# Decoder block on one core: the feed-forward's seven products regrouped, their sums kept in PSUM, and the last output row cut 512, 256, 256

## The chip, the core and the metric

One NeuronCore of a Trainium2 chip runs the whole program; the other cores are idle. The metric is the device time of one execution in microseconds. Before the change it was 758.20 us, the median of three runs (758.01 to 758.51). Lower is better. The output is compared with the reference in float32.

## What is computed

One decoder block on x of 512 tokens by 1024 channels. Cut to what matters here:

```
p   = x @ W_in + b_in                      # projections for two token mixers and their gates
m   = sigmoid(g_A) * y_A + sigmoid(g_B) * y_B   # y_A: gated mixing in chunks, y_B: gated linear attention
h   = layer_norm(alpha * x + m @ W_out)
f   = square(relu(h @ W_ff1)) @ W_ff2      # 1024 -> 4096 -> 1024
out = layer_norm(alpha * h + f)
```

The change is in the feed-forward, above all in the product with `W_ff2`, and in two small places beside it.

## The kernel before

**Every float32 product is three passes.** `split` (L88) writes a number as a rounded part `hi` (ScalarE's cast, L89) and a rest `lo` (VectorE's subtraction, L90). TensorE then sums hi·hi, hi·lo and lo·hi in one PSUM bank (`passes`, L196). Weights come in chunks of 128x1024 (512 KB), one DMA each on SyncE's queue (L111), into raw buffers, and are split into `wh` and `wl`, which have seven buffers each (`W_BUFS`), so that splitting runs up to seven chunks ahead of TensorE. `load_to`, `sum_to` and `split_to` (L102 to L143) drive this along a list of chunks that `_stream` (L1114) writes out.

**The stages, in order.** The first q and k products on the `head` array (L272); a small low-rank product `pa` whose weights are the tile `als` (L283 to L290, L327); the projections for u, v, q, k, the gates and the two mixers (up to about 365 us); the output projection and the first layer norm; from about 412 us the feed-forward.

**The feed-forward.** Hidden units come in 8 blocks of 512. A hidden job (`hidden`, L918) is 24 matmuls of 512 columns, and ScalarE squares its relu into the tile `F`. Two blocks make a pair: `F` then holds a 512-token by 1024-hidden matrix a, cut in 2 by 2 quarters, a(i,j) with i the token half and j the hidden block; the matching rows of `W_ff2` are cut in quarters b(i,j), i the hidden block and j the output half. For the first three pairs (`PAIRS`) the product a·b is made of seven products of quarters instead of eight (Strassen's scheme). `operand` (L935) makes the sum of quarters of a that a product needs, in the tile `d`, and splits it into `oh`, `ol`; `sum_to` makes the sums of quarters of b in place in the raw buffers (L124). Each product is 24 matmuls of 512 columns (L986), 12 for each half t of its 256 tokens. TensorE's order is written out: a hidden job of the next pair, a product, a hidden job, a product, and so on. `keep` (L955) takes each product out of PSUM into an SBUF sum of its own, `acc[m]`: for the first pair a ScalarE copy (L961), or VectorE with alpha·h added (L959); for later pairs a VectorE addition (L963). `together` (L993) combines the seven sums into the four quarters of the output `bufB`, partly among the last products, partly among the output pieces.

**The end.** The fourth pair is an ordinary product (L1077): for each of four 128-token rows, pieces of 512 and 512 columns, and for the last row pieces of 512, 384 and 128 columns. Each piece is 24 matmuls, then VectorE adds it to `bufB` (L1078) and takes the statistics (L1079). When a row is complete follow the aggregate (L1084), the reciprocal root on GpSimd (L1086), four operations for the layer norm (L1089, L1093) and two DMAs out.

**What sets the order.** TensorE, VectorE, ScalarE and GpSimd run in the order in which the program's functions issue instructions, except in the first stage, where only TensorE is fixed and the other engines are ordered by the framework. SyncE's queue is always ordered by the framework, and waits at its head hold up what stands behind. A tile that takes over another's memory waits until that one is done with.

Of the kernel before, what the change touches and what calls it, by code (L numbers as in the profile page):

```python
# [15 lines left out]
P = 128  # L16
# [30 lines left out]
def hybrid_block(  # L47
# [50 lines left out]
    raws, chunks, kept = {}, {}, {}  # L98
    lanes, ring = {0: rpool}, {lane: [] for lane in LANES}
    state = {"load": 0, "sum": 0, "split": 0}  # L100

    def load_to(n):  # L102
        while state["load"] < min(n, NCHUNK):
            i = state["load"]
            kind, lane, key, news = STREAM[i]
            if news is not None:
                ends = ring[lane]
                if len(ends) >= LANES[lane] and ends[-LANES[lane]] >= state["split"]:
                    break
                raw = lanes[lane].tile([P, 1024], F32, name=f"raw{i}", tag="raw")  # L110
                nc.sync.dma_start(raw, w_all[news])  # L111
                kept.setdefault(key, []).append(raw)
                users = [j for j in range(i + 1, NCHUNK) if STREAM[j][2] == key]
                users = [j for n_, j in enumerate(users) if all(STREAM[x][3] is None for x in users[:n_])]
                ends.append(max([i] + (users if key else [])))
            raws[i] = kept[key][-1:] if kind == "one" else kept[key][-2:]
            state["load"] = i + 1

    def sum_to(n):
        while state["sum"] < min(n, state["load"]):  # L120
            i = state["sum"]
            raw, *other = raws[i]
            if other:
                nc.vector.tensor_tensor(raw, raw, other[0], op=ALU.add if STREAM[i][0] == "sum" else ALU.subtract)  # L124
            state["sum"] = i + 1

    def split_to(n):
        n += n > ASIDE
        while state["split"] < min(n, NCHUNK):
            i = state["split"]  # L130
            load_to(i + 1)
            if i != ASIDE:
                hi = wpool.tile([P, 1024], F32R, name=f"wh{i}", tag="wh")
                lo = wpool.tile([P, 1024], F32R, name=f"wl{i}", tag="wl")
            else:
                hi, lo = (a[:, 4:6, :].rearrange("p k t -> p (k t)") for a in (xh, xl))
            sum_to(i + 2)
            raw = raws[i][0]
# [4 lines left out]
        load_to(n + sum(LANES.values()) if 1 in lanes else n + RAW_BUFS)  # L143

# [105 lines left out]
    for i in range(4):  # L250
        raws[i] = [None]
# [31 lines left out]
    als_ = gt.tile([P, 1536], F32R, name="als", tag="qt", bufs=QT_BUFS)  # L283
    nc.vector.memset(als_.bitcast(F32), 0.0)
    als = []
    for k, o in enumerate(ALS_AT):
        als.append(als_[:, 192 * k + o : 192 * k + o + P])
        a4 = als[k].rearrange("p (r m) -> p r m", r=4)
        split(a4[:, 0, 0:RANK], a4[:, 3, 0:RANK], wal[:, k, :])
        nc.scalar.copy(a4[:, 1:3, 0:RANK], a4[:, 0:1, 0:RANK].bitcast(F32).broadcast_to([P, 2, RANK]))  # L290
# [32 lines left out]
    def low_rank():  # L323
        pa = ps_a.tile([P, 512], F32, name="pa", tag="aux")
        for k in range(KT):
            for i, xx in enumerate((xh, xl)):
                nc.tensor.matmul(  # L327
                    pa, als[k], xx[:, k, :], start=(k == 0 and i == 0), stop=(k == KT - 1 and i == 1)
                )
# [573 lines left out]
    xp = pool(tail, "xp", side="right")  # L903
    acc = {m: xp.tile([P, 2, 512], F32, name=f"acc{m}") for m in (1, 2, 5)}
    quarter = lambda a, i, j: a[:, 2 * i : 2 * i + 2, 512 * j : 512 * j + 512]
    for m, i, j in ((7, 0, 0), (3, 0, 1), (4, 1, 0), (6, 1, 1)):
        acc[m] = quarter(bufB, i, j)
    fp = pool(tail, "fp", side="right", bufs=2)
    seven = ExitStack()
    lanes[1] = pool(seven, "rpool2", side="right", bufs=LANES[1])  # L910
    op = pool(seven, "op", side="left", bufs=2)
    sub = lambda o, x_, y_: nc.vector.tensor_tensor(o, x_, y_, op=ALU.subtract)  # L912
# [21 lines left out]

    def operand(F, p, m):  # L935
        a = lambda i, j: F[:, j - 1, :, (i - 1) * 256 : i * 256]
        x_, *y_ = {
            5: (a(1, 2), a(1, 1)),
            1: (a(1, 1), a(2, 2)),
            3: (a(1, 1),),  # L940
            4: (a(2, 2),),
            6: (a(2, 1), a(1, 1)),
            7: (a(1, 2), a(2, 2)),
            2: (a(2, 1), a(2, 2)),
        }[m]
        if y_:
            d_ = op.tile([P, 4, 256], F32, name=f"d{p}_{m}", tag="d", bufs=1)
            sub(d_, x_, y_[0])
            x_ = d_
# [5 lines left out]
    def keep(p, m, t, ps):  # L955
        dst = acc[m][:, t, :]
        if p == 0 and m in (6, 7):
            h = quarter(bufA, *((1, 1) if m == 6 else (0, 0)))[:, t, :]
            nc.vector.scalar_tensor_tensor(dst, h, ALPHA, ps, op0=ALU.mult, op1=ALU.add)  # L959
        elif p == 0:  # L960
            nc.scalar.copy(dst, ps)  # L961
        else:
            nc.vector.tensor_add(dst, dst, ps)  # L963

    made = {}

    def seven_products(F, p, F_next):
# [4 lines left out]
        def job(n):  # L972
            m = ORDER[n]
# [4 lines left out]
            hi, lo = made.pop((p, n))  # L978
            u0 = take_chunks(2)
            for t in range(2):  # L980
                tsl = slice(t * P, (t + 1) * P)
                ps = ps_m.tile([P, 512], F32, name=f"m{p}_{m}_{t}", tag="ps")
                for k in range(4):
                    wh, wl = (c.rearrange("p (k n) -> p k n", k=2)[:, k % 2, :] for c in chunks[u0 + k // 2])
                    for i, (s_, m_) in enumerate(passes(hi[:, k, tsl], lo[:, k, tsl], wh, wl)):
                        nc.tensor.matmul(ps, s_, m_, start=(k == 0 and i == 0), stop=(k == 3 and i == 2))  # L986
                    if t and k % 2:
                        split_to(u0 + k // 2 + 1 + W_BUFS)
                keep(p, m, t, ps)
# [3 lines left out]
    def together(m, t, terms, h=None):  # L993

        z = acc[m][:, t, :]
        for sign, n in terms:
            nc.vector.tensor_tensor(z, z, acc[n][:, t, :], op=ALU.add if sign > 0 else ALU.subtract)
        if h:
            nc.vector.scalar_tensor_tensor(
                z, quarter(bufA, *h)[:, t, :], ALPHA, z, op0=ALU.mult, op1=ALU.add  # L1000
            )
# [35 lines left out]
    for n, product in enumerate(seven_products(F, PAIRS - 1, None)):  # L1037
# [6 lines left out]
        if ORDER[n] == 4:  # L1044
            together(7, 0, ((1, 4),))
        if ORDER[n] == 1:
            together(7, 0, ((1, 1),))
# [4 lines left out]
    together(7, 0, ((-1, 5),))  # L1052
    later = {
        (0, 0): [(6, 0, ((1, 3),)), (3, 0, ((1, 5),), (0, 1))],
        (0, 1): [(7, 1, ((1, 4), (1, 1), (-1, 5))), (6, 1, ((1, 3),)), (3, 1, ((1, 5),), (0, 1))],
        (1, 0): [(4, t, ((1, 2),), (1, 0)) for t in range(2)],
        (1, 1): [(6, t, ((1, 1), (-1, 2))) for t in range(2)],
    }
# [7 lines left out]
    for t in range(NT):  # L1066
        tsl = slice(t * P, (t + 1) * P)
        row, z = bufA[:, t, :], bufB[:, t, :]
        pieces = ((0, 512), (512, 512)) if t < NT - 1 else ((0, 512), (512, 384), (896, 128))
        for pi, (c0, n) in enumerate(pieces):  # L1070
# [9 lines left out]
            for part in later.get((t, pi), ()):  # L1080
                together(*part)
# [32 lines left out]
def _stream():  # L1114
# [4 lines left out]
    out = [("one", 0, None, None)] * 4 + [("one", 0, None, c) for c in range(n)]  # L1119
# [3 lines left out]
    take = lambda k: [("one", 0, None, next(f1_jobs)) for _ in range(k)]  # L1123

    def operand(p, m, h):
        b = lambda i, j: f2 + 8 * p + 2 * (2 * (i - 1) + j - 1) + h
        kind, c = {
            2: ("one", b(1, 1)),
            6: ("sum", b(1, 2)),
            3: ("sum", b(2, 2)),  # L1130
            5: ("one", None),
            7: ("sum", b(2, 1)),
            4: ("sum", b(1, 1)),
            1: ("less", b(2, 2)),
        }[m]
        return (kind, h, (p, h), c)
# [6 lines left out]
    out += [("one", 0, None, f2 + 8 * PAIRS + c) for c in range(8 * (DF // 1024 - PAIRS))]  # L1143
# [81 lines left out]
```

## Time and profile before

| | |
|---|---|
| median of three runs | 758.20 us |
| the profiled execution | 757.96 us, of which 756.2 us from first to last instruction |
| TensorE busy | 747.2 us, 3498 matmuls |
| VectorE busy | 492.8 us, 618 instructions |
| ScalarE busy | 349.5 us, 472 instructions |
| mean granted TensorE clock | 0.997 |

The page's first part gives each engine's busy time and its share of the span. A row of the timeline gives the start of an instruction, its duration, the engine, the line, and output<-inputs with the shape. For TensorE the duration of one matmul is longer than the distance from one start to the next, since matmuls are pipelined; the distance is what counts for the time. A row of the chain of work that ended last gives the start, the length of the stretch, the engine, what it worked on, and how many instructions. A row of the waits gives who waited for whom, the total, how often, and the longest.

### The profile page before, as it was taken

The numbers are of one execution on the slowest core, as the hardware profiler recorded it, in microseconds if no ns is written. First come the engines' busy times: TensorE is split into PE (matmuls) and PEld (weight loads), VectorE is DVE, ScalarE is ACT, GpSimd is POOL, SyncE is SP. The second block draws the span as 40 slices with busy tenths as digits, with TensorE's granted clock in tenths as the row PEclk, the third lists the DMA queues.
The fourth block names the chain that finished last, engine by engine and source line by source line (L and its number), as shares of the span: only waits on it lengthen the run. The fifth ranks groups of instructions, "written<-read, shape, count | busy, mean of one in ns | idle before, by whom it ended". The sixth has DMA issues, their size and how long they took to land.

```text
span 756.2 us, 8829 instructions
## 1 busy us (share of the span) xinstructions
PE 747.2 (99%) x3498; PEld 626.8 (83%) x3498; DVE 492.8 (65%) x618; ACT 349.5 (46%) x472; POOL 29.8 (4%) x60
## 2 busy tenths in 40 slices
PE   9999999999999999999999999999999999999996
PEld 7878888888888888888888988888888888888885
DVE  8478876676575554435458544874677667777995
ACT  7475744363254735444222544454644444445300
POOL 1000000000000102000002000000000000000011
PEclk9999999999999999999999999999999999999998
DMA  8623422222142131432341423444234333534111
GB/s 341 208 73 125 137 77 80 84 84 84 36 141 75 56 126 56 144 107 84 98 158 33 171 62 107 139 140 140 86 137 141 137 112 112 164 114 166 58 56 55
DMA packets 25465, 85.15 MB, mean 113 GB/s; under 512 B 3088, under 2 KB 3344, under 8 KB 25424
## 3 DMA queue, kind: packets, MB, share of 16 engines
q1 hardware_dynamic: 25280, 84.33, 32.4%
q8 instruction: 27, 0.44, 0.2%
q10 hardware_dynamic: 144, 0.26, 0.1%
q14 instruction: 14, 0.11, 0.1%
HBM read 82.48 MB, written 2.10 MB: 112 GB/s over the span
## 4 chain that ended last, share of the span: by engine, by line
PE 96%; issue 1%; DVE 1%; DMA 0%; POOL 0%; DVEq 0%; POOLq 0%
PE f L691 22%; PE ps L213 17%; PE m L986 15%; PE f L1077 6%; PE gb L691 6%; PE r L691 6%; PE ga L691 6%; PE u L691 6%; PE qk L691 3%; PE first L272 3%; PE sc L519 2%; PE pm L744 1%; PE po L553 1%; PE po L557 1%; PE po L555 1%
## 5 line engine op out<-in xcount | busy, mean ns | idle before, releaser
L90 DVE TENSOR_TENSOR wl<-raw,wh 128x1024 fp32r<-128x1024 f32 x141 | 171.2, 1222 | 99.2 <-ACT wh L89 97.7
L89 ACT CAST wh<-raw 128x1024 fp32r<-128x1024 f32 x141 | 145.7, 1044 | 51.1 <-PE ps L213 23.7
L691 PE MATMUL f<-xh,wh 128*128 128x512 f32 (+1 forms) x288 | 105.4, 366 | 0.0
L691 PE MATMUL f<-xl,wh 128*128 128x512 f32 (+1 forms) x288 | 105.3, 365 | 0.0
L691 PE MATMUL f<-xh,wl 128*128 128x512 f32 (+1 forms) x288 | 105.2, 365 | 0.0
L986 PE MATMUL m<-wh,oh 128*128 128x512 f32 x168 | 65.4, 389 | 0.0
L986 PE MATMUL m<-wl,oh 128*128 128x512 f32 x168 | 65.4, 389 | 0.0
L986 PE MATMUL m<-wh,ol 128*128 128x512 f32 x168 | 65.4, 389 | 0.0
L691 PEld LDWEIGHTS f<-xh,wl 128*128 128x128 f32 x288 | 54.3, 189 | 8.8
L691 PEld LDWEIGHTS f<-xh,wh 128*128 128x128 f32 x288 | 54.3, 189 | 8.7
L691 PEld LDWEIGHTS f<-xl,wh 128*128 128x128 f32 x288 | 54.3, 189 | 8.6
L213 PE MATMUL ps<-wh,xh 128*128 128x512 f32 x128 | 50.4, 394 | 0.0
L213 PE MATMUL ps<-wh,xl 128*128 128x512 f32 x128 | 49.8, 389 | 0.0
L213 PE MATMUL ps<-wl,xh 128*128 128x512 f32 x128 | 49.8, 389 | 0.0
L915 ACT ACTIVATE F<-f 128x512 f32<-128x512 f32 (+1 forms) x28 | 15.0, 536 | 70.7 <-PE f L691 70.7
L124 DVE TENSOR_TENSOR raw<-raw,raw 128x1024 f32<-128x1024 f32 x30 | 36.6, 1221 | 9.1 <-DMA raw<-in_w_all 9.1
L986 PEld LDWEIGHTS m<-wh,ol 128*128 128x128 f32 x168 | 31.5, 188 | 6.6
L986 PEld LDWEIGHTS m<-wh,oh 128*128 128x128 f32 x168 | 31.5, 188 | 6.6
L986 PEld LDWEIGHTS m<-wl,oh 128*128 128x128 f32 x168 | 31.5, 188 | 6.5
L89 ACT CAST oh<-d 128x1024 fp32r<-128x1024 f32 x15 | 15.7, 1049 | 36.4 <-DVE d L912 36.4
L90 DVE TENSOR_TENSOR ol<-d,oh 128x1024 fp32r<-128x1024 f32 x15 | 18.4, 1225 | 16.7 <-ACT oh L89 16.7
L213 PEld LDWEIGHTS ps<-wh,xl 128*128 128x128 f32 x128 | 24.0, 188 | 5.1
(231 smaller groups left out, 1477.1 us busy)
## 6 DMA issues: line engine op xcount, KB each, us to landing
raw<-in_w_all SPq DMA_DIRECT2D x136, 512.0 KB, 3.3
bufB<-in_head SPq DMA_DIRECT2D x4, 512.0 KB, 7.9
xr<-in_x SPq DMA_DIRECT2D x8, 256.0 KB, 3.6
out<-bufA SPq DMA_DIRECT2D x8, 256.0 KB, 2.0
bufA<-in_head SPq DMA_DIRECT2D x3, 512.0 KB, 5.3
brow<-in_b_in SPq DMA_DIRECT2D x4, 256.0 KB, 6.4
g<-in_ln_g SPq DMA_DIRECT2D x2, 512.0 KB, 4.0
b<-in_ln_b SPq DMA_DIRECT2D x2, 512.0 KB, 4.9
```

The costliest lines, as they stand in the source:

```text
L89: nc.scalar.copy(hi, src)
L90: nc.vector.tensor_tensor(lo, src, hi.bitcast(F32), op=ALU.subtract)
L124: nc.vector.tensor_tensor(raw, raw, other[0], op=ALU.add if STREAM[i][0] == "sum" else ALU.subtract)
L213: nc.tensor.matmul(ps, s_, m_, start=(k == 0 and i == 0), stop=(k == KT - 1 and i == 2))
L272: nc.tensor.matmul(first[e], s_, m_[:, k, :], start=(k == 0 and i == 0), stop=(k == KT - 1 and i == 2))
L519: nc.tensor.matmul(sc[:, c, 0:192], pr.kt[:, jc * P : (jc + 1) * P], pr.qt[:, jc, :], start=True, stop=True)
L553: nc.tensor.matmul(po, pr.AT[:, j, c, :], vs, start=True, stop=(c == 0))
L555: nc.tensor.matmul(po, pr.QI[:, j, c * P : (c + 1) * P], pr.S[j], start=False, stop=True)
L691: nc.tensor.matmul(ps, s_, m_, start=(k == 0 and i == 0), stop=(k == KT - 1 and i == 2))
L915: nc.scalar.activation(dst, ps, AF.Relu)
L986: nc.tensor.matmul(ps, s_, m_, start=(k == 0 and i == 0), stop=(k == 3 and i == 2))
L1077: nc.tensor.matmul(ps, s_, m_, start=(f == 0 and i == 0), stop=(f == 7 and i == 2))
```

## The change

**Another form of the seven products.** The order of the products becomes 1, 2, 5, 6, 3, 7, 4 (`ORDER`), and with it what each multiplies (Winograd's scheme). On a's side four sums are made in place in one tile `d`: s1 = a(2,1)+a(2,2) for product 5, s2 = s1-a(1,1) for 6, s4 = a(1,2)-s2 for 3, s3 = a(1,1)-a(2,1) for 7; products 1, 2 and 4 take a(1,1), a(1,2) and a(2,2) as they are. On b's side t1 = b(1,2)-b(1,1) for 5, t2 = b(2,2)-t1 for 6, b(2,2)-b(1,2) for 7, b(2,1)-t2 for 4; products 1, 2 and 3 take b(1,1), b(2,1) and b(2,2).

**Kept raw weights.** Four tiles A0, A1, B0, B1 (`held`; 0 and 1 are the halves of a quarter) keep b(1,1), t1 and t2, and b(2,2), across products; the rest of the loads share three raw buffers. A pair still loads 12 chunks of `W_ff2`: b(1,2) and b(2,1) twice. Product 3 needs no load; before, it was product 5.

**Two accumulators in PSUM.** Products 1, 6, 7, 4 are summed one on top of the other in the two banks `mx`, products 5 and 3 in the two banks `mv`; product 2 has banks of its own. After each product VectorE adds the state of its accumulator to one quarter of `bufB`; for the first pair products 1, 5, 6 and 4 bring alpha·h along. The separate sums `acc` in SBUF and all of `together` are gone, and ScalarE copies nothing out any more. A product that goes on in an accumulator may only start when VectorE has read it for the product before.

**Beside it.** The low-rank weights `als` are built in one of the `wh` buffers by fewer, larger instructions. The last row's pieces are 512, 256, 256. The memory reserved for descriptors that GpSimd would write is cut to 1024 bytes a partition, which makes room for the four kept tiles.

```diff
-ORDER = (2, 6, 3, 7, 4, 1, 5)
+ORDER = (1, 2, 5, 6, 3, 7, 4)
...
+            _, own, dst, _, less = STREAM[i]
+            if dst is not None:
+                raw = held[dst]
+                if less:
+                    x_, y_ = (held[a] if a else kept[i] for a in less)
+                    nc.vector.tensor_tensor(raw, x_, y_, op=ALU.subtract)
+                kept[i] = raw
...
-    als_ = gt.tile([P, 1536], F32R, name="als", tag="qt", bufs=QT_BUFS)
-    nc.vector.memset(als_.bitcast(F32), 0.0)
-    als = []
-    for k, o in enumerate(ALS_AT):
-        als.append(als_[:, 192 * k + o : 192 * k + o + P])
-        a4 = als[k].rearrange("p (r m) -> p r m", r=4)
-        split(a4[:, 0, 0:RANK], a4[:, 3, 0:RANK], wal[:, k, :])
-        nc.scalar.copy(a4[:, 1:3, 0:RANK], a4[:, 0:1, 0:RANK].bitcast(F32).broadcast_to([P, 2, RANK]))
+    als = wpool.tile([P, KT, 4, 32], F32R, name="als", tag="wh")
+    nc.vector.memset(als.bitcast(F32), 0.0)
+    split(als[:, :, 0, 0:RANK], als[:, :, 3, 0:RANK], wal)
+    for r_ in (1, 2):
+        nc.scalar.copy(als[:, :, r_, 0:RANK], als[:, :, 0, 0:RANK].bitcast(F32))
...
+    def accumulators(m, name):
+        if m in (1, 6, 7, 4):
+            if m == 1:
+                x_ = ps_s.tile([P, 2, 512], F32, name=f"mx{name}", tag="sc")
+                sums["x"] = [x_[:, t, :] for t in range(2)]
+            return sums["x"], m == 1
+        if m in (5, 3):
+            if m == 5:
+                sums["v"] = [ps_a.tile([P, 512], F32, name=f"mv{name}_{t}", tag="aux") for t in range(2)]
+            return sums["v"], m == 5
+        return [ps_m.tile([P, 512], F32, name=f"m{name}_{t}", tag="ps") for t in range(2)], True
...
+                    nc.tensor.matmul(
+                        ps,
+                        s_,
+                        m_,
+                        start=(begins and k == 0 and i == 0),
+                        stop=(k == 3 and i == 2),
+                        skip_group_check=True,
+                    )
...
+            dst = quarter(bufB, *GOES[m])[:, t, :]
+            if p == 0 and m in NEW:
+                h = quarter(bufA, *GOES[m])[:, t, :]
+                nc.vector.scalar_tensor_tensor(dst, h, ALPHA, ps, op0=ALU.mult, op1=ALU.add)
+            else:
+                nc.vector.tensor_add(dst, dst, ps)
...
-        pieces = ((0, 512), (512, 512)) if t < NT - 1 else ((0, 512), (512, 384), (896, 128))
+        pieces = ((0, 512), (512, 512)) if t < NT - 1 else ((0, 512), (512, 256), (768, 256))
...
-    nc = bacc.Bacc("TRN2", target_bir_lowering=False, num_devices=1)
+    nc = bacc.Bacc("TRN2", target_bir_lowering=False, num_devices=1, dynamic_dma_scratch_size=1024)
```

Three places show what moves. The first is VectorE in the third pair. Before, this is the stretch around product 3: the rest `wl` of a chunk, the operand of product 7 (`d_7`, `ol_7`), product 3 taken out in two halves, and among them sums and rests of later chunks.

```order
L90 TENSOR_TENSOR wl_5005<-raw_4851,wh_5004 128x1024
L912 TENSOR_TENSOR d_7_5013<-F_4195 128x1024
L90 TENSOR_TENSOR ol_7_5016<-d_7_5013,oh_7_5015 128x1024
L963 TENSOR_TENSOR bufB<-bufB,m_3_0_5019 128x512
L90 TENSOR_TENSOR wl_5041<-raw_4884,wh_5040 128x1024
L124 TENSOR_TENSOR raw_4932<-raw_4932,raw_5011 128x1024
L90 TENSOR_TENSOR wl_5053<-raw_5009,wh_5052 128x1024
L963 TENSOR_TENSOR bufB<-bufB,m_3_1_5033 128x512
```

After the change this is the stretch around product 7 of the third pair, on whose accumulator `mx` product 4 goes on after one hidden job:

```order
L88 TENSOR_TENSOR wl_5173<-raw_5100,wh_5172 128x1024
L88 TENSOR_TENSOR ol_4_5179<-F_4149,oh_4_5178 128x1024
L991 TENSOR_TENSOR bufB<-bufB,mx_1_4799 128x512
L88 TENSOR_TENSOR wl_5202<-raw_5130,wh_5201 128x1024
L88 TENSOR_TENSOR wl_5214<-raw_5142,wh_5213 128x1024
L991 TENSOR_TENSOR bufB<-bufB,mx_1_4799 128x512
```

Here neither a sum of a's quarters nor a sum of b's quarters stands before the accumulator is read. The second place is VectorE's end, the last row's pieces, with `f_3_...` the pieces by their first column. Before:

```order
L1078 TENSOR_TENSOR bufB<-bufB,f_3_512_5631 128x384
L1079 BN_STATS st_3_2367<-bufB 128x6
L1078 TENSOR_TENSOR bufB<-bufB,f_3_896_5658 128x128
L1079 BN_STATS st_3_2367<-bufB 128x6
L1084 BN_AGGR mv_l_5685<-st_3_2367 128x2
```

After:

```order
L1073 TENSOR_TENSOR bufB<-bufB,f_3_512_5537 128x256
L1074 BN_STATS st_3_2347<-bufB 128x6
L1073 TENSOR_TENSOR bufB<-bufB,f_3_768_5564 128x256
L1074 BN_STATS st_3_2347<-bufB 128x6
L1077 BN_AGGR mv_l_5591<-st_3_2347 128x2
```

Only the widths differ, and with them the widths of the 48 matmuls in front. The third place is SyncE's queue early in the program, where the first layer norm's two rows `g` and `b` (broadcast to 128 partitions) now stand among the chunk loads; before, they stood some 45 rows further on. Before, the place reads:

```order
L111 DMA raw_385<-in_w_all 128x1024
L111 DMA raw_387<-in_w_all 128x1024
L111 DMA raw_429<-in_w_all 128x1024
L111 DMA raw_431<-in_w_all 128x1024
L111 DMA raw_534<-in_w_all 128x1024
```

After:

```order
L116 DMA raw_365<-in_w_all 128x1024
L116 DMA raw_367<-in_w_all 128x1024
L179 DMA g_2352<-in_ln_g 128x1024
L179 DMA b_2354<-in_ln_b 128x1024
L116 DMA raw_409<-in_w_all 128x1024
L116 DMA raw_411<-in_w_all 128x1024
L116 DMA raw_514<-in_w_all 128x1024
```

The two rows moved ahead, and every chunk load behind them is two places later in the queue.

More of the change, by code (lines that the diff above doesn't have):

```diff
@@ L36 @@
 RAW_BUFS = 3
-LANES = {0: RAW_BUFS, 1: 2}
 PAIRS = 3
-ORDER = (2, 6, 3, 7, 4, 1, 5)
+ORDER = (1, 2, 5, 6, 3, 7, 4)
 LEVELS = (32, 8, 2)
-ALS_AT = (0, 4, 48, 24, 12, 40, 56, 2)
 WARM = 9
@@ L96, in hybrid_block @@
     ASIDE = NCHUNK - 3
-    raws, chunks, kept = {}, {}, {}
-    lanes, ring = {0: rpool}, {lane: [] for lane in LANES}
+    chunks, kept, ring = {}, {}, []
+    held, held_to = {}, {}
     state = {"load": 0, "sum": 0, "split": 0}
@@ L104, in load_to @@
             i = state["load"]
[L105 to L108, printed above, removed]
+            c, own, *_ = STREAM[i]
+            if c is not None and own is None:
+                if len(ring) >= RAW_BUFS and ring[-RAW_BUFS] >= state["split"]:
                     break
[L110 to L116, printed above, removed]
+                kept[i] = rpool.tile([P, 1024], F32, name=f"raw{i}", tag="raw")
+                ring.append(i)
+            elif c is not None:
+                if "pool" not in held or held_to.get(own, -1) >= state["split"]:
+                    break
+                kept[i] = held[own] = held["pool"].tile([P, 1024], F32, name=f"raw{i}", tag=own)
+                held_to[own] = max(j for j in range(i, min(i + 40, NCHUNK)) if STREAM[j][3] == STREAM[i][3] and own in STREAM[j][2:])
+            if c is not None:
+                nc.sync.dma_start(kept[i], w_all[c])
             state["load"] = i + 1
@@ L121, in sum_to @@
             i = state["sum"]
-            raw, *other = raws[i]
-            if other:
-                nc.vector.tensor_tensor(raw, raw, other[0], op=ALU.add if STREAM[i][0] == "sum" else ALU.subtract)
+            _, own, dst, _, less = STREAM[i]
[5 more added lines that the diff above has]
+                kept[i] = raw
             state["sum"] = i + 1
@@ L137, in split_to @@
             sum_to(i + 2)
-            raw = raws[i][0]
+            raw = kept.pop(i, None)
             if raw is not None:
@@ L142, in split_to @@
             state["split"] = i + 1
-        load_to(n + sum(LANES.values()) if 1 in lanes else n + RAW_BUFS)
+        load_to(n + RAW_BUFS + 2)
     xh = xpool.tile([P, KT, T], F32R, name="xh")
@@ L248, in hybrid_block @@
         nc.tensor.matmul(wu[:, :P], ones, ones, start=True, stop=True)
-    for i in range(4):
-        raws[i] = [None]
     state["load"], state["sum"] = 4, 4
@@ L327, in low_rank @@
                 nc.tensor.matmul(
-                    pa, als[k], xx[:, k, :], start=(k == 0 and i == 0), stop=(k == KT - 1 and i == 1)
+                    pa, als[:, k].rearrange("p r m -> p (r m)"), xx[:, k, :], start=(k == 0 and i == 0), stop=(k == KT - 1 and i == 1)
                 )
@@ L895, in hybrid_block @@
     )
-    xp = pool(tail, "xp", side="right")
-    acc = {m: xp.tile([P, 2, 512], F32, name=f"acc{m}") for m in (1, 2, 5)}
     quarter = lambda a, i, j: a[:, 2 * i : 2 * i + 2, 512 * j : 512 * j + 512]
-    for m, i, j in ((7, 0, 0), (3, 0, 1), (4, 1, 0), (6, 1, 1)):
-        acc[m] = quarter(bufB, i, j)
     fp = pool(tail, "fp", side="right", bufs=2)
     seven = ExitStack()
-    lanes[1] = pool(seven, "rpool2", side="right", bufs=LANES[1])
+    held["pool"] = pool(seven, "held", side="right")
     op = pool(seven, "op", side="left", bufs=2)
-    sub = lambda o, x_, y_: nc.vector.tensor_tensor(o, x_, y_, op=ALU.subtract)
     def square_to(dst, ps):
@@ L933, in take_raw @@
         return lambda e, tsl, ps: square_to(F[:, j, e, tsl], ps)
+    GOES = {1: (0, 0), 2: (0, 0), 5: (1, 1), 6: (0, 1), 3: (0, 1), 7: (1, 1), 4: (1, 0)}
+    NEW = (1, 5, 6, 4)
+    made, sums = {}, {}
     def operand(F, p, m):
         a = lambda i, j: F[:, j - 1, :, (i - 1) * 256 : i * 256]
[L937 to L949, printed above, removed]
+        if m == 5:
+            made["d"] = op.tile([P, 4, 256], F32, name=f"d{p}", tag="d", bufs=1)
+        if m in (1, 2, 4):
+            src = a(*{1: (1, 1), 2: (1, 2), 4: (2, 2)}[m])
+        else:
+            src = d_ = made["d"]
+            x_, y_ = {5: (a(2, 1), a(2, 2)), 6: (d_, a(1, 1)), 3: (a(1, 2), d_), 7: (a(1, 1), a(2, 1))}[m]
+            nc.vector.tensor_tensor(d_, x_, y_, op=ALU.add if m == 5 else ALU.subtract)
@@ L950, in operand @@
         hi = op.tile([P, 4, 256], F32R, name=f"oh{p}_{m}", tag="oh")
         lo = op.tile([P, 4, 256], F32R, name=f"ol{p}_{m}", tag="ol")
-        split(hi, lo, x_)
+        split(hi, lo, src)
         return hi, lo
[L955 to L963, printed above, removed]
@@ L965, in hybrid_block @@
-    made = {}
+    def accumulators(m, name):
[5 more added lines that the diff above has]
+        if m in (5, 3):
+            if m == 5:
+                sums["v"] = [ps_a.tile([P, 512], F32, name=f"mv{name}_{t}", tag="aux") for t in range(2)]
+            return sums["v"], m == 5
+        return [ps_m.tile([P, 512], F32, name=f"m{name}_{t}", tag="ps") for t in range(2)], True
@@ new lines, in product_of @@
+    def product_of(name, m, ops, take):
+        hi, lo = ops
+        u0 = take_chunks(2)
+        banks, begins = accumulators(m, name)
+        for t, ps in enumerate(banks):
+            tsl = slice(t * P, (t + 1) * P)
+            for k in range(4):
+                wh, wl = (c.rearrange("p (k n) -> p k n", k=2)[:, k % 2, :] for c in chunks[u0 + k // 2])
+                for i, (s_, m_) in enumerate(passes(hi[:, k, tsl], lo[:, k, tsl], wh, wl)):
+                    nc.tensor.matmul(
[6 more added lines that the diff above has]
+                    )
+                if t and k % 2:
+                    split_to(u0 + k // 2 + 1 + W_BUFS)
+            take(m, t, ps)
@@ L967, in seven_products, with keep, f @@
+    def keep(p):
+        def f(m, t, ps):
+            dst = quarter(bufB, *GOES[m])[:, t, :]
+            if p == 0 and m in NEW:
+                h = quarter(bufA, *GOES[m])[:, t, :]
+                nc.vector.scalar_tensor_tensor(dst, h, ALPHA, ps, op0=ALU.mult, op1=ALU.add)
+            else:
+                nc.vector.tensor_add(dst, dst, ps)
+        return f
     def seven_products(F, p, F_next):
@@ L972, in job @@
         def job(n):
-            m = ORDER[n]
             if n < 6:
@@ L977, in job @@
                 made[p + 1, 0] = operand(F_next, p + 1, ORDER[0])
[L978 to L989, printed above, removed]
-        return [lambda n=n: job(n) for n in range(7)]
[L993 to L1001, printed above, removed]
+            product_of(f"{p}_{ORDER[n]}", ORDER[n], made.pop((p, n)), keep(p))
+        return [lambda n=n: job(n) for n in range(7)]
     F = fp.tile([P, 2, 4, T], F32, name="F0", tag="F")
@@ L1043, in hybrid_block @@
         product()
[L1044 to L1047, printed above, removed]
         if n == 5:
@@ L1051, in hybrid_block @@
     split_to(NCHUNK)
[L1052 to L1058, printed above, removed]
     seven.close()
@@ L1079, in hybrid_block @@
             nc.vector.bn_stats(st2[t][:, pi, :], z[:, sl])
-            for part in later.get((t, pi), ()):
-                together(*part)
         mv = lnp.tile([P, 2], F32, name=f"mv_l2{t}", tag="mv", bufs=4)
@@ L1118, in _stream @@
     n = 15 * 4
-    out = [("one", 0, None, None)] * 4 + [("one", 0, None, c) for c in range(n)]
+    out = [(None, None, None, None, None)] * 4 + [(c, None, None, None, None) for c in range(n)]
     f1 = n
@@ L1122, in _stream @@
     f1_jobs = iter(range(f1, f2))
-    take = lambda k: [("one", 0, None, next(f1_jobs)) for _ in range(k)]
+    take = lambda k: [(next(f1_jobs), None, None, None, None) for _ in range(k)]
     def operand(p, m, h):
         b = lambda i, j: f2 + 8 * p + 2 * (2 * (i - 1) + j - 1) + h
[L1127 to L1134, printed above, removed]
+        A, B = f"A{h}", f"B{h}"
+        c, own, dst, less = {
+            1: (b(1, 1), A, A, None),
+            2: (b(2, 1), None, None, None),
+            5: (b(1, 2), None, A, (None, A)),
+            6: (b(2, 2), B, A, (B, A)),
+            3: (None, None, B, None),
+            7: (b(1, 2), None, B, (B, None)),
+            4: (b(2, 1), None, A, (None, A)),
         }[m]
-        return (kind, h, (p, h), c)
+        return (c, own, dst, p, less)
     out += take(8)
@@ L1142, in _stream @@
             out += take(1 + (i == 0)) + product
-    out += [("one", 0, None, f2 + 8 * PAIRS + c) for c in range(8 * (DF // 1024 - PAIRS))]
+    out += [(f2 + 8 * PAIRS + c, None, None, None, None) for c in range(8 * (DF // 1024 - PAIRS))]
     return out
```

## The prediction

> **What bounds the kernel now.** I read the page first, its busy times and its chain of work that ended last:
>
> ```profile
> PE 747.2 (99%) x3498; PEld 626.8 (83%) x3498; DVE 492.8 (65%) x618; ACT 349.5 (46%) x472; POOL 29.8 (4%) x60
> PE 96%; issue 1%; DVE 1%; DMA 0%; POOL 0%; DVEq 0%; POOLq 0%
> ```
>
> TensorE is busy for 99% of the span and makes 96% of the chain. [...] All its waits on other engines:
>
> ```profile
> PE wu L248 <- POOL bal L294: 1.1, 1, 1.1
> PE pt L408 <- PE ps L213: 0.6, 1, 0.6
> PE first L272 <- ACT xh L262: 0.3, 1, 0.3
> PE sd L493 <- DVE dt L484: 0.2, 1, 0.2
> ```
>
> That is 2.2 us in the whole program, and none of it in the feed-forward. The chain in order of time gives the rhythm there, product (`m`), hidden job (`f`), product, down to the fourth pair:
>
> ```profile
> 655.60 5.44 PE m L986 x24
> ...
> 699.12 5.44 PE m L986 x24
> 704.56 44.95 PE f L1077 x216
> ```
>
> 24 matmuls take 5.44 us, 0.2267 us each, and each stretch begins where the one before ends. The busy times by stretch (us and count of PE, PEld, DVE, ACT, POOL; granted clock; DMA) for the three pairs say the same:
>
> ```profile
> 460.00:541.40 81.40, 81.40 (x360) 67.39 (x360) 53.32 (x47) 42.86 (x55) 0.00 (x0) 1.00 0.36 123
> 541.40:623.00 81.60, 81.60 (x361) 67.57 (x360) 58.60 (x56) 39.29 (x48) 0.00 (x0) 1.00 0.38 129
> 623.00:704.50 81.50, 81.50 (x361) 67.48 (x360) 63.00 (x65) 42.73 (x55) 0.00 (x0) 1.00 0.42 139
> ```
>
> TensorE fills them, at full clock. VectorE, which the new form relieves, is at 66 to 77%. So the big part of the change works on an engine that nobody waits for; it can lose time here, but hardly win any. The change leaves TensorE's 3498 matmuls in number and order, and all their widths but the last 48.
>
> **The last pieces: the one term on the path.** Now 384 and 128 columns, then 256 and 256. First the old pieces' first matmuls and the very last one; then the start and the end of the program's other 24 matmuls of 256 columns in three passes, a half hidden job:
>
> ```profile
> 742.52 0.33 PE L1077 MATMUL f<-wh,Fs 128*128 128x384 f32 x1
> 746.71 0.22 PE L1077 MATMUL f<-wh,Fs 128*128 128x128 f32 x1
> 749.22 0.28 PE L1077 MATMUL f<-wh,xl 128*128 128x128 f32 x1
> 412.61 0.28 PE L691 MATMUL f<-xh,wh 128*128 128x256 f32 x1
> 415.36 0.28 PE L691 MATMUL f<-xh,wl 128*128 128x256 f32 x1
> ```
>
> 384 columns: 746.71 - 742.52 = 4.19 us for 24, 0.175 each. 128 columns: from 746.71 to the last start 2.51 us over 23 distances, 0.109 each, though a third of the columns. 256 columns: 2.75 over 23, 0.1196 each. Narrow matmuls hit a floor near 0.11. Before, from the first start to the last end: 749.50 - 742.52 = 6.98 us. After: 47 distances of 0.1196 and one duration of 0.28 = 5.90 us. That is **-1.08 us**.
>
> [...]
>
> Behind the last matmul VectorE adds and takes statistics, now 256 columns wide:
>
> ```profile
> 746.90 0.56 DVE L1078 TENSOR_TENSOR bufB<-bufB,f 128x384 f32<-128x384 f32 x1 [2.77 <-PE f L1077]
> 747.50 0.56 DVE L1079 BATCH_NORM_STATS2 st<-bufB 128x6 f32<-128x384 f32 x1
> 749.53 0.29 DVE L1078 TENSOR_TENSOR bufB<-bufB,f 128x128 f32<-128x128 f32 x1 [1.48 <-PE f L1077]
> 749.86 0.29 DVE L1079 BATCH_NORM_STATS2 st<-bufB 128x6 f32<-128x128 f32 x1
> ```
>
> Midway between 0.29 and 0.56 lies 0.425, twice 0.135 more: **+0.27 us**. The first 256 piece's two operations (0.85) are done long before the second's 2.87 us end. The aggregate, the root, the layer norm and the stores after that are the same. Sum: **-0.81 us**.
>
> **The new form.** What VectorE and ScalarE gain and lose:
>
> ```profile
> L124 DVE TENSOR_TENSOR raw<-raw,raw 128x1024 f32<-128x1024 f32 x30 | 36.6, 1221 | 9.1 <-DMA raw<-in_w_all 9.1
> L912 DVE TENSOR_TENSOR d<-F 128x1024 f32<-128x1024 f32 x15 | 18.3, 1218 | 0.0
> L963 DVE TENSOR_TENSOR bufB<-bufB,m 128x512 f32<-128x512 f32 x16 | 10.9, 680 | 0.0
> L997 DVE TENSOR_TENSOR bufB<-bufB,acc 128x512 f32<-128x512 f32 x12 | 8.2, 687 | 0.2
> L997 DVE TENSOR_TENSOR bufB<-bufB 128x512 f32<-128x512 f32 x4 | 2.7, 679 | 0.0
> L999 DVE SCALAR_TENSOR_TENSOR bufB<-bufA,bufB 128x512 f32<-128x512 f32 x4 | 2.8, 692 | 0.1
> ```
>
> Weight sums 30 to 24: -6 x 1.22 = -7.3. Operand sums 15 to 12: -3.7. `together` gone: -8.2 - 2.7 - 2.8 = -13.7. Ten ScalarE copies of the first pair become VectorE additions: +10 x 0.68 = +6.8. Net -17.9 us of VectorE, hidden by TensorE's unbroken rhythm: **0**. The first pair alone carries more (+6.8, less 1.22 for each of two weight and one operand sum, +3.1 on 53.3 in 81.4 us), still below the third pair's 63.0 before.
>
> What is new is a wait. A product that goes on in an accumulator waits for VectorE's reading of the one before, and VectorE's queue (rests of chunks, sums) stands ahead of that reading. The shortest way is 7 to 4: half t of product 4 starts half a product and a hidden job after half t of 7 ended, 2.72 + 5.44 = 8.16 us. How late does VectorE read today? The worst is product 3 of the third pair (655.60 to 661.04 above, halves ending at 658.32 and 661.04):
>
> ```profile
> 662.49 0.68 DVE L963 TENSOR_TENSOR bufB<-bufB,m 128x512 f32<-128x512 f32 x1
> 666.49 0.68 DVE L963 TENSOR_TENSOR bufB<-bufB,m 128x512 f32<-128x512 f32 x1
> ```
>
> Read out by 663.17 and 667.17, that is 4.85 and 6.13 us after the halves ended, with an operand sum and a weight sum ahead. Around product 7 now stands neither: minus 1.22 for `d`, and 1.22 for the sum. So I take 3 to 5 us against a cover of 8.16: **0**, upper bound below. From 6 to 7, from 5 to 3 and on to the next pair's 1 there is at least another hidden job.
>
> The tightest place before is the last chunk's rest:
>
> ```profile
> 706.88 2.35 DVE L90 TENSOR_TENSOR wl<-raw,wh 128x1024 fp32r<-128x1024 f32 x2
> ```
>
> It is done at 709.23; the fourth pair's first piece needs it at its 23rd matmul, 704.56 + 22 x 0.2267 = 709.55. Cover 0.3 us. Ahead of it VectorE loses an operand sum (1.22) and an addition of `together` (0.69), gains nothing, so the cover grows. Product 4's two loads, where 5 had none, come seven chunks ahead, over 20 us.
>
> **Early edits.** `als` is cleared later, among the first splits, with 1024 columns instead of 1536:
>
> ```profile
> 1.17 1.34 DVE L284 MEMSET als<- 128x1536 f32 x1 [1.17 <-PEq L1214]
> 12.63 0.69 DVE L90 TENSOR_TENSOR xl<-bufB,xh 128x512 fp32r<-128x512 f32 x1
> 21.98 0.39 PE L272 MATMUL first<-xh,wh 128*128 128x512 f32 x1
> 20.31 0.34 ACT L290 CAST als<-als 128x32 fp32r<-128x32 f32 x2
> 27.42 0.39 PE L327 MATMUL pa<-xh,als 128*128 128x512 f32 x1
> ```
>
> Some 0.9 us (1.34 x 1024/1536) go in ahead of the seventh k tile's `xl` at 12.63, which TensorE uses from 21.98: hidden. `als` itself was ready at 20.65 for 27.42, and takes fewer instructions now: **0**. The `wh` buffer that it borrows is free again when `pa` ends, and six others remain. The two layer-norm rows move ahead on SyncE's queue:
>
> ```profile
> g<-in_ln_g SPq DMA_DIRECT2D x2, 512.0 KB, 4.0
> b<-in_ln_b SPq DMA_DIRECT2D x2, 512.0 KB, 4.9
> 54.56 2.94 ACT L89 CAST wh<-raw 128x1024 fp32r<-128x1024 f32 x3
> 79.62 10.89 PE u L691 x48
> ```
>
> At worst the chunks behind come 8.9 us later. These are split from 54.56 on, for `u` products from 79.62: 25 us of cover: **0**. In their old place the queue now holds the first kept tiles' loads, which wait for memory as `g` and `b` did. Bounds for all early edits together: 0.5 us either way, since stage borders cost TensorE 0.2 to 0.6 us a time in the waits above and could shift.
>
> **Sum.** The profiled execution took 757.96 us, 0.24 below the median: 757.96 - 0.81 = 757.15, and on the median's scale **757.4 us**. That is 0.1% faster, within the 0.2% (1.5 us) that a measurement of this kernel can tell from no change.
>
> **Rivals.**
> - *The narrow pieces give nothing* (0.08). In the tail the moving operand is the weights, in the rows of 256 it was the activations; if 256 lies at the mean of 384 and 128, 0.142, TensorE's time stays and the +0.27 is left: 758.5. Against it: 512 columns take 0.2267 with either operand moving. [...]
> - *A wait in place of the SBUF sums: slower* (0.11). If VectorE reads product 7 later than 8.16 us after a half, product 4 stands, in each of the three pairs. At twice today's worst, 12.26, that is 3 x 4.1 = 12.3 us: 769.7. For it: a wait per product that was not there, and VectorE's rests stand in line ahead. Against it: the line ahead of 7's reading is shorter than the one that gave 6.13. It decides the sign from a lag of 8.4 us, and the 0.2% from about 8.9.
> - *More room removes old waits* (0.05). If the 0.6, 0.3 and 0.2 us that TensorE waits inside the program go as well: 757.4 - 1.1 = 756.3.
> - *VectorE was the bound, and its 17.9 us count* (0.01): 739.5. The stretches without a wait speak against it.
>
> The forecast keeps 0.75. **Range:** the forecast with its 0.5 us is 756.9 to 757.9; the first rival takes it up to 758.5, and the spread of the runs to 758.8; below I allow 756.7. Outside are the other rivals, 0.17. Faster by over 0.2% (under 756.7): 0.07; slower by over 0.2% (over 759.7): 0.12; within: 0.81.
>
> **What would show it.** The chain's last `f` stretch of 216 matmuls is 43.9 instead of 44.95 us; the last two additions and statistics take 0.42 each; products and hidden jobs stay at 5.44, with no row of `m` among TensorE's waits; VectorE's busy time falls to some 473 us. A row "PE m <- DVE" of more than 1 us in total, or distances of 0.14 in the last pieces, would prove me wrong.

## The result, and the profile after

The changed kernel took **812.55 us**, the median of five runs (812.1 to 813.22), against 758.20 before: ratio 1.0718, 95% interval 1.0701 to 1.0735. It is slower by 54 us. The forecast was 757.4 with a range of 756.7 to 758.8. The prediction was wrong: it spoke of no change, and of a range far below. The profiled execution took 812.1 us, of which 810.3 from first to last instruction; before it was 756.2. One of the five runs of the kernel before took 1080.9 us and stands apart; the other four lie between 757.96 and 758.51.

The page of the changed kernel, busy times and chain:

```profile
PE 762.0 (94%) x3498; PEld 634.0 (78%) x3498; DVE 474.4 (59%) x592; ACT 344.2 (42%) x449; POOL 29.9 (4%) x60
PE 87%; DVE 6%; ACT 3%; issue 2%; DMA 0%; POOL 0%; DVEq 0%; POOLq 0%
```

VectorE does 18 us less, as forecast. But the chain, of which TensorE made 96% before, now runs through VectorE and ScalarE for 9% of the span. The waits of TensorE (who waits for whom, total us, times, longest):

```profile
PE mx L972 <- DVE bufB L991: 29.0, 9, 4.9
PE mx L972 <- DVE bufB L989: 10.0, 3, 4.9
PE wu L252 <- POOL bal L293: 1.1, 1, 1.1
PE pt L407 <- PE ps L217: 0.6, 1, 0.6
PE first L274 <- ACT xh L264: 0.3, 1, 0.3
PE sd L492 <- DVE dt L483: 0.2, 1, 0.2
```

The four old waits stand as they were. New are 12 waits of 39.0 us, all on the accumulator `mx`, four in each of three pairs, none on `mv` or `m`. Where they stand is told by the chain in order of time (start, length, what, how many instructions):

```profile
470.71 0.61 ACT F L911
471.87 1.04 ACT wh L87
472.94 1.23 DVE wl L88
474.17 1.14 DVE ol L88
475.95 4.34 PE mx L972 x12
480.29 5.44 PE f L690 x24
485.73 5.44 PE m L972 x24
...
754.87 4.62 PE mx L972 x12
759.49 43.85 PE f L1072 x216
```

A product of `mx` stands in the chain with 12 matmuls, where one of `m` has 24: the chain reaches its **second half** through VectorE, and its first half is off the chain. The timeline around product 1 of the first pair (start, duration, engine, instruction, and in brackets the idle time before it with what ended it):

```profile
473.00 0.39 PE L972 MATMUL mx<-wh,ol 128*128 128x512 f32 x1
474.08 1.22 DVE L88 TENSOR_TENSOR ol<-F,oh 128x1024 fp32r<-128x1024 f32 x1
475.22 0.68 DVE L989 SCALAR_TENSOR_TENSOR bufB<-bufA,mx 128x512 f32<-128x512 f32 x1
475.95 0.29 PEld L972 LDWEIGHTS mx<-wh,oh 128*128 128x128 f32 x1 [2.98 <-DVE bufB L989]
475.95 0.79 PE L972 MATMUL mx<-wh,oh 128*128 128x512 f32 x1 [2.56 <-DVE bufB L989]
```

The last matmul of the first half ends at 473.39. VectorE has a chunk's rest `wl` and the next operand's `ol` in its queue, and reads the half out by 475.90. Only then does TensorE begin the second half, though that goes into the other bank. Product 1 begins `mx` afresh and waits like the others.

Two things make up the loss. Added up over the 504 product matmuls, the distances from start to start are 169.1 us against 114.24 before, 54.9 more. Of these 41.0 lie in the 12 distances that hold a wait: 39.0 of waiting and 0.17 each of starting again. Another 13.6 lie in matmuls behind a pause, the first at up to 0.59 us and most of the next at 0.427, not at 0.227. Less 1.08 for the last pieces, plus 0.27 for VectorE at the end, that makes 54.1, the difference of the spans.

### The profile page after: what moved, and what is told of

Read it like the earlier page. It is cut to its first block, busy times and chain, and to the rows that moved or that the text cites. A ratio compares the mean times of both kernels' runs of the same rounds, so it can differ in the third digit from the quotient of the medians.

```text
span 810.3 us, 8780 instructions
## 1 busy us (share of the span) xinstructions
PE 762.0 (94%) x3498; PEld 634.0 (78%) x3498; DVE 474.4 (59%) x592; ACT 344.2 (42%) x449; POOL 29.9 (4%) x60
## 4 chain that ended last, share of the span: by engine, by line
PE 87%; DVE 6%; ACT 3%; issue 2%; DMA 0%; POOL 0%; DVEq 0%; POOLq 0%
PE f L690 21%; PE ps L217 15%; PE mx L972 6%; PE f L1072 5%; PE r L690 5%; PE gb L690 5%; PE ga L690 5%; PE u L690 5%; PE mv L972 4%; PE qk L690 3%; PE first L274 3%; PE m L972 2%; PE sc L518 2%; DVE wl L88 2%; DVE ol L88 2%
## 5 line engine op out<-in xcount | busy, mean ns | idle before, releaser
L972 PE MATMUL mx<-wh,oh 128*128 128x512 f32 x96 | 44.3, 461 | 39.1 <-DVE bufB L991 29.0
L972 PEld LDWEIGHTS mx<-wh,oh 128*128 128x128 f32 x96 | 21.2, 221 | 48.5 <-DVE bufB L991 32.8
L972 PE MATMUL mx<-wl,oh 128*128 128x512 f32 x96 | 42.0, 438 | 0.0
L972 PE MATMUL mx<-wh,ol 128*128 128x512 f32 x96 | 41.8, 435 | 0.0
L127 DVE TENSOR_TENSOR raw<-raw,raw 128x1024 f32<-128x1024 f32 x24 | 29.3, 1219 | 2.6 <-DMA raw<-in_w_all 2.6
L217 PEld LDWEIGHTS ps<-wl,xh 128*128 128x128 f32 x128 | 24.0, 188 | 4.9
L217 PEld LDWEIGHTS ps<-wh,xh 128*128 128x128 f32 x128 | 24.0, 188 | 4.8
L690 PE MATMUL u<-xh,wh 128*128 128x512 f32 x64 | 25.9, 405 | 0.0
L690 PE MATMUL ga<-xh,wh 128*128 128x512 f32 x64 | 25.9, 404 | 0.0
```

The lines of the kernel that those rows point to most:

```text
L127: nc.vector.tensor_tensor(raw, x_, y_, op=ALU.subtract)
L972: nc.tensor.matmul(ps, s_, m_, start=(begins and k == 0 and i == 0), stop=(k == 3 and i == 2), skip_group_check=True,)
```

## The experiments

Three theories. **A**: the wait is kept by the tile. The two halves of `mx` are two banks of one tile (`x_` in the diff), so a write to the second waits for the reading of the first. **B**: accumulating makes it; a product on top of another waits for the reading between. **C**: VectorE's queue reaches the readings too late, and TensorE pays for that whatever holds the sums. The kernel before, run again beside them, had a median of 757.89 us (beside the first four) and 758.08 (beside the last three).

**Two tiles.** The halves of `mx` become two tiles of one bank each. The memory of the tile of two banks, which earlier stages use, is given back first to make room for them; those lines are left out here.

```diff
...
-                x_ = ps_s.tile([P, 2, 512], F32, name=f"mx{name}", tag="sc")
-                sums["x"] = [x_[:, t, :] for t in range(2)]
+                sums["x"] = [ps_x.tile([P, 512], F32, name=f"mx{name}_{t}", tag=f"mx{t}") for t in range(2)]
```

> The changed kernel with one thing undone: the two halves of the accumulator mx are two tiles of one bank each, no longer one tile of two banks. The accumulations, the raw weights and the queue of VectorE stay. Theory A (a write to the second bank waits for the reading of the first because both belong to one tile): all 12 waits go, and with them the lowered clock behind them; the seven products return to 5.44 us each, and the time is 758.2 - 0.8 = 757.4 us (756.7 to 758.8). Theory B (a product that accumulates on top of another waits for the reading between them, whatever the tile): the accumulation is unchanged, so the 39.0 us of waits stay and the time stays near 812.6. Theory C (VectorE's queue reaches the readings too late, and TensorE pays for that whichever tile holds the sums): VectorE's queue is unchanged, so again near 812.6.

Measured: **757.07 us**, ratio to before 0.9988 (0.9979 to 0.9997). All of TensorE's waits in this run:

```profile
PE wu L253 <- POOL bal L294: 1.1, 1, 1.1
PE pt L408 <- PE ps L218: 0.6, 1, 0.6
PE sd L493 <- DVE dt L484: 0.2, 1, 0.2
```

Product 1 of the first pair again, with the end of the first half, the first two matmuls of the second, and VectorE's reading:

```profile
472.71 0.39 PE L974 MATMUL mx<-wh,ol 128*128 128x512 f32 x1
472.94 0.39 PE L974 MATMUL mx<-wh,oh 128*128 128x512 f32 x1
473.17 0.39 PE L974 MATMUL mx<-wl,oh 128*128 128x512 f32 x1
...
474.93 0.68 DVE L991 SCALAR_TENSOR_TENSOR bufB<-bufA,mx 128x512 f32<-128x512 f32 x1
```

VectorE reads as late as before, 2.5 us behind the half's end (475.61 against 473.10), and works in the same order. But TensorE goes straight on, and writes one bank while VectorE reads the other. A holds; B and C forecast no change and fall.

**Both readings behind both halves.** One tile, but read at the end of the product:

```diff
-            take(m, t, ps)
+            if m not in (1, 6, 7, 4):
+                take(m, t, ps)
+        if m in (1, 6, 7, 4):
+            for t, ps in enumerate(banks):
+                take(m, t, ps)
```

> The changed kernel, mx still one tile of two banks, but in the products 1, 6, 7 and 4 both readings are issued behind the matmuls of both halves, and not each behind its own half. Theory A: the second half has no reading in front of it any more, the 12 waits between the halves go, and a new one could only stand between two mx products (the next write to the tile behind the last reading), where there are at least 8.16 us for a lag of 3 to 6: 757.4 us (756.7 to 760). Theory B: the accumulation is as it was, and the waits stay, at the next mx product: near 812. Theory C: VectorE has the same work, and its readings come no earlier; near 812.

Measured: **757.33 us**, ratio 0.9991 (0.9982 to 1.0). No wait on `mx`; TensorE's list has the same three waits as the run above. So it isn't the wide tile by itself, but a reading issued between two writes to it. And a wait from one product to the next, the one that the prediction had priced, does not show: the cover between products suffices.

**Swapped tiles.** `mx` in two tiles of one bank, `mv` (products 5 and 3) in the tile of two:

```diff
-                sums["x"] = [x_[:, t, :] for t in range(2)]
+                sums["x"] = [ps_a.tile([P, 512], F32, name=f"mx{name}_{t}", tag="aux") for t in range(2)]
...
-                sums["v"] = [ps_a.tile([P, 512], F32, name=f"mv{name}_{t}", tag="aux") for t in range(2)]
+                v_ = ps_s.tile([P, 2, 512], F32, name=f"mv{name}", tag="sc")
+                sums["v"] = [v_[:, t, :] for t in range(2)]
```

> The changed kernel with the tiles of the accumulators swapped: mx lies in two tiles of one bank, and mv, with its products 5 and 3, in the one tile of two banks. Theory A: the waits follow the tile. None in mx; one between the halves of each of the products 5 and 3, that is 6 instead of 12, each about as long as the ones now (39.0 us over 12 is 3.3, the longest 5.1), so 16 to 30 us, and some of the lowered clock (14.7 us for 12 now, 5 to 10 here): 757.4 + 20 to 40 = 778 to 797 us. Theory B: the waits stay with mx, four a pair, near 812. Theory C: the time stays near 812 too, since VectorE's queue is the same.

Measured: **800.36 us**, ratio 1.0559 (1.0545 to 1.0574). TensorE's waits on the accumulators in this run:

```profile
PE mv L972 <- DVE bufB L991: 24.5, 5, 4.9
PE mv L972 <- DVE bufB L989: 4.9, 1, 4.9
```

The waits have moved with the tile: six, on `mv`, none on `mx`. The time is 3 us above what I gave for A, because all six are of the long kind. Behind 5 and 3 come the products 6 and 7, whose operands need the sum `d` besides `ol`, and both stand ahead of the reading. VectorE's queue itself waits there too: in the changed kernel's product 6, 1.1 us between `d` and `ol` for ScalarE's `oh`. The slow matmuls behind the pauses cost some 12 us more: in the chain the 12 matmuls behind a pause take 4.38 to 5.49 us, where those of product 7 in the changed kernel, at whole clock, take 3.02.

**The pieces alone.** The kernel before with one line changed:

```diff
-        pieces = ((0, 512), (512, 512)) if t < NT - 1 else ((0, 512), (512, 384), (896, 128))
+        pieces = ((0, 512), (512, 512)) if t < NT - 1 else ((0, 512), (512, 256), (768, 256))
```

> The kernel before with the last output row's pieces 512, 256, 256 alone, and the old products. The prediction's term: 12 matmul distances fewer of 0.175 or 0.109 us in PE's favour, 1.08 us, less 0.27 us for the longer last addition: 758.2 - 0.8 = 757.4 us. If the term is as said, the chain's last stretch of f is 43.9 us and not 44.95. If narrow pieces cost only by their columns, 758.2 to 758.5.

Measured: **757.01 us**, ratio 0.9988 (0.9979 to 0.9997). The chain's last stretch and VectorE's last two operations on the pieces:

```profile
704.68 43.87 PE f L1077 x216
```

```profile
748.57 0.42 DVE L1078 TENSOR_TENSOR bufB<-bufB,f 128x256 f32<-128x256 f32 x1 [1.99 <-PE f L1077]
749.03 0.43 DVE L1079 BATCH_NORM_STATS2 st<-bufB 128x6 f32<-128x256 f32 x1
```

44.95 has become 43.87, and 0.29 has become 0.42: both as forecast. (The 48 matmuls stay 48; their distances are shorter in sum, where the expectation speaks of 12 fewer.) The median is 0.88 below that of before, where 0.81 was forecast. The kernel with two tiles, which has this and all the rest of the change, stands at 757.07: the seven products' new form gives and costs nothing that can be measured.

**Operand late.** In the changed kernel the next product's operand is issued behind the product:

```diff
+            product_of(f"{p}_{ORDER[n]}", ORDER[n], made.pop((p, n)), keep(p))
             if n < 6:
                 made[p, n + 1] = operand(F, p, ORDER[n + 1])
             elif p < PAIRS - 1:
                 made[p + 1, 0] = operand(F_next, p + 1, ORDER[0])
-            product_of(f"{p}_{ORDER[n]}", ORDER[n], made.pop((p, n)), keep(p))
```

> The changed kernel, mx still one tile of two banks with each half read behind its own matmuls; only the next product's operand (d and ol on VectorE, 1.1 to 1.2 us each) is issued behind the product and not ahead of it, so that VectorE's queue holds less ahead of a reading. Theory A: the wait stands where it stood, 12 times, and only its length changes, since it is the time VectorE takes to come to the reading and to finish it: the pauses of 2.7 and 5.1 us lose ol and d and fall to the reading of 1.2 us and some 0.4 us of passing on, about 1.7 us each. 12 x 1.7 = 20 us, and pauses this short should leave the clock up: 757.4 + 20 = 778 us (773 to 785; more if an operand now comes late for its own product, which would show as a wait at a product's first matmuls). A theory by which VectorE's queue alone is the cause would have the waits go altogether: 757 to 760.

Measured: **795.38 us**, ratio 1.0495 (1.0477 to 1.0512), above what I expected. TensorE's waits in the feed-forward of this run:

```profile
PE mx L972 <- DVE bufB L991: 12.7, 9, 4.6
PE mx L972 <- DVE bufB L989: 3.6, 3, 1.4
PE mx L972 <- DVE ol L88: 3.2, 6, 0.5
PE mv L972 <- DVE ol L88: 3.2, 6, 0.5
PE mx L972 <- ACT oh L87: 2.1, 3, 0.7
PE mv L972 <- ACT oh L87: 2.1, 3, 0.7
```

The 12 waits on readings remain and shrink from 39.0 to 16.3 us: the queue sets how long a wait is, not whether there is one. (A reading takes 0.68 us in this run; in the changed kernel TensorE goes on 0.05 us behind it, 475.90 to 475.95. The expectation had put 1.2 and 0.4.) The miss is 17 us. New waits make 10.6 of it: an operand made this late isn't ready for its own product. Counted by distances the products and the borders to them lose 37.6 us; 26.9 are the waits, and the rest is starting again, 30 times, and one stretch of slow matmuls behind the longest wait (12 take 4.62 us in the chain, the other second halves there 3.01 to 3.04). These 10.7 us the expectation put at nothing.

**One tile, in the kernel before.** Nothing accumulates here from product to product; only product 7's halves are put into one tile:

```diff
-                ps = ps_m.tile([P, 512], F32, name=f"m{p}_{m}_{t}", tag="ps")
+                if m == 7:
+                    if t == 0:
+                        x_ = ps_s.tile([P, 2, 512], F32, name=f"m7{p}", tag="sc")
+                    ps = x_[:, t, :]
+                else:
+                    ps = ps_m.tile([P, 512], F32, name=f"m{p}_{m}_{t}", tag="ps")
```

> The kernel before (each product in sums of its own, nothing accumulated from product to product, the old last pieces), with one thing added: the two halves of product 7 lie in one tile of two banks, and not in two tiles. Theory A: the tile alone brings the wait: 3 waits, one in each pair of chunks, between the halves of product 7, each 2.5 to 5.1 us long as VectorE comes to the reading, with a lowered clock behind some: 758.2 + 8 to 20 = 766 to 778 us, and a row of TensorE waiting for VectorE on that tile. Theory B (the accumulation makes the wait): nothing accumulates here, so no wait, 757.9 to 758.5.

Measured: **768.32 us**, ratio 1.0142 (1.0126 to 1.0157). TensorE's waits for VectorE in the feed-forward of this run:

```profile
PE m L991 <- DVE bufB L963: 5.6, 2, 2.9
PE m L991 <- DVE bufB L959: 2.6, 1, 2.6
```

Three waits, one a pair. The tile alone makes them, without any accumulation. B falls a second time.

**Filled pauses.** The changed kernel with idle matmuls between the halves, into a bank that nobody reads:

```diff
+            if t and m in (1, 6, 7, 4):
+                spare = ps_m.tile([P, 512], F32, name=f"fill{name}", tag="ps")
+                w0 = chunks[u0][0].rearrange("p (k n) -> p k n", k=2)[:, 0, :]
+                for _ in range(22 if m == 6 else 12):
+                    nc.tensor.matmul(spare, hi[:, 0, tsl], w0, start=True, stop=True)
```

> The changed kernel with its 12 waits left in place, and idle matmuls put into them: between the two halves of the products 1, 7 and 4 twelve matmuls of 512 columns, 12 x 0.227 = 2.7 us, of product 6 twenty-two, 5.0 us, into a bank that nobody reads. They add 9 x 2.72 + 3 x 4.99 = 39.5 us of work to TensorE, as much as the waits of 39.0 us held. It tells the two parts of the loss apart. If the 427 ns distances behind the pauses come from TensorE having stood idle, they go, and the waits with them, and the time is 812.6 - 14.7 = 798 us (795 to 801), with a clock of 0.997 and more. If they come from something else about these products (the reading of the neighbouring bank, the operands), the time stays near 812 and the distances of 427 ns stay. If TensorE does not wait but is slowed by VectorE's reading itself, the fill adds its 39.5 us on top: 850.

Measured: **800.09 us**, ratio 1.0556 (1.054 to 1.0571). In this run's waits the one left on `mx`, and from its busy times by stretch two stretches of 3.41 us inside product 6 of the first pair (us; busy PE, PEld, DVE, ACT, POOL; granted clock; DMA):

```profile
PE mx L977 <- DVE bufB L996: 1.1, 1, 1.1
```

```profile
509.60:513.01 3.41, 3.41 (x17) 2.83 (x16) 2.29 (x3) 1.05 (x1) 0.00 (x0) 1.00 0.92 356
513.01:516.42 3.41, 3.41 (x16) 2.56 (x15) 1.01 (x2) 0.65 (x1) 0.00 (x0) 1.00 0.07 29
```

The idle work fits into the waits and the clock stays up: no distance of 0.427 is left in the products. Against the changed kernel that is 12.5 us less, although TensorE does 39.5 us more. So the slow matmuls come from TensorE having stood idle, and the loss splits into some 41 us of pauses and 12 to 13 of lowered clock.

## Why the prediction was wrong

**What bounds the kernel: right for before.** The unbroken rhythm of 5.44 us is there again wherever the wait is taken away: with two tiles the span is 755.2, and TensorE waits for 1.9 us in all.

**The last pieces: right.** -1.08 and +0.27 came as 44.95 to 43.87 and 0.29 to 0.42. The rival that they give nothing (758.5) falls. Had the time gone by the columns alone, 384 and 128 being as many as 256 and 256, the stretch would have stayed at 44.95. The new pieces' matmuls stand 0.1198 us apart in the changed kernel, where the prediction put 0.1196; what keeps the 128 columns at 0.109 was not shown. The prediction took its price from 24 matmuls of 256 columns and called them the program's only others; there are 192, and the 24 are one half hidden job of eight.

**VectorE's work and the early edits: right.** 474.4 us where some 473 were forecast, the old waits unchanged, the cover of the last chunk kept. All this leaves the time alone, as said.

**The failed step** is the one on the new wait: "A product that goes on in an accumulator waits for VectorE's reading of the one before", with the shortest way from 7 to 4 and a cover of 8.16 us. No run shows that wait: the cover suffices, in the kernel that reads behind both halves too. But the step looked only from product to product. It took from the code that accumulators are what is new, and did not ask which instructions share a tile. `mx` was made as one tile of two banks, `mv` and `m` as two tiles. So there is a nearer wait, from one half of a product to the next, with no cover at all: the second half follows the first at once. Its size could have been had from the working itself. VectorE's lag behind a half was put at 3 to 5 us; it is 2.5 us at product 1 (475.90 - 473.39), and in product 6 as long as the longest wait there, 4.9. That lag was held against 8.16 us, and belonged against nothing, 12 times: 39.0 us of waits. The slow matmuls behind the waits, 13.6 us, were no term of the sum at all.

**The slower rival** (769.7) had the right kind of mechanism, VectorE's lag in the chain, but the wrong place, product 4 alone, and a lag of 8.4 us that VectorE never came near: in the changed kernel it is done with the two halves of product 7 of the first pair 2.5 and 2.95 us after they end. Three waits where there were twelve, and no word of the clock. It was given 0.11, and the range left it out.

**The test named in the prediction worked.** "A row 'PE m <- DVE' of more than 1 us in total" was to prove it wrong; the rows are there, under the name `mx`.

## What to carry to other kernels

When sums move into a shared tile, list for every write what else is read or written in that tile between it and the write before, and price each wait by the reader's whole queue and by what that queue waits for; the bank that a write touches didn't matter here, the tile did. Where two halves are read one by one, give them a tile each, or issue the readings behind both: either took the 54 us back and left the 0.1% of the last pieces. When one engine makes nearly the whole chain, as TensorE here with 96%, taking work off another can hardly gain, so a change of this kind is to be searched for new waits above all.

## What the runs showed of the hardware

Some of the pauses cost more than their length, and some did not. The changed kernel in stretches of 3.41 us, around product 1, product 6 and product 7 of the first pair (us; busy PE, PEld, DVE, ACT, POOL; granted clock; DMA):

```profile
472.03:475.44 3.41, 1.36 (x6) 0.78 (x5) 2.50 (x3) 1.82 (x2) 0.00 (x0) 1.00 0.33 126
475.44:478.86 3.42, 2.91 (x7) 2.33 (x8) 0.46 (x1) 0.00 (x0) 0.00 (x0) 0.50 0.00 0
478.86:482.27 3.41, 3.41 (x17) 2.81 (x16) 2.27 (x2) 2.11 (x2) 0.00 (x0) 1.00 0.00 0
...
509.60:513.01 3.41, 0.61 (x3) 0.18 (x1) 2.36 (x2) 0.98 (x2) 0.00 (x0) 0.99 0.87 306
513.01:516.42 3.41, 1.31 (x3) 1.12 (x4) 1.82 (x2) 0.19 (x1) 0.00 (x0) 0.50 0.35 132
516.42:519.84 3.42, 3.42 (x9) 2.68 (x9) 0.68 (x1) 1.04 (x1) 0.00 (x0) 0.51 0.00 0
519.84:523.25 3.41, 3.41 (x16) 2.79 (x16) 3.41 (x5) 1.05 (x1) 0.00 (x0) 1.00 0.59 162
...
536.88:540.29 3.41, 2.48 (x11) 1.70 (x10) 1.38 (x2) 2.90 (x4) 0.00 (x0) 1.00 0.57 187
540.29:543.71 3.42, 1.79 (x8) 1.49 (x9) 1.57 (x2) 0.10 (x1) 0.00 (x0) 1.00 0.49 158
543.71:547.12 3.41, 3.41 (x17) 2.83 (x16) 2.28 (x2) 2.01 (x2) 0.00 (x0) 1.00 0.00 0
```

The borders are set so that the slow matmuls behind product 1 end at one, 478.86; the same step of 3.413 us then meets the end of the slow matmuls behind product 6, 519.84, twelve steps on. All seven such ends in this run lie on that grid, the last 82 steps on, at 758.75; (758.75 - 478.86) / 82 = 3.413. The trace's record of the granted clock has it at half seven times up to there, four times for 3.413 us and three times for 6.827. In these rows the clock of a stretch is whole or half (0.99 and 1.00, 0.50 and 0.51). It is half in the stretch that follows one in which TensorE was busy for 40% or less (1.36, 0.61 and 1.31 of 3.41), and whole behind one with 52% (1.79). So the two pauses of 2.95 us, from start to start, at product 1 and product 7 differ: the first falls mostly into one stretch, the second is cut in two by a border, and costs no clock.

In this run the most that TensorE was busy in a stretch with half clock behind it is 1.36 us, the least with whole clock behind it 1.68 (553.93 to 557.34, product 4 of the first pair); where between them the line lies was not shown. In the kernel before with one tile, too, the length of the pause alone doesn't decide: its three waits are 2.6 to 2.9 us long, and the 12 matmuls behind them take 3.06, 3.03 and 4.33 us in the chain.
